# One-hot matrices of the gates: two tokens innermost instead of four

## The chip, the cores and the metric

The kernel runs on one core of a Trainium2 chip. The metric is the device time of one execution in microseconds (us); the lower the better. The kernel before takes 3132.16 us (median of 3 runs, 3129.18 to 3136.56).

## The reference, cut to what matters

The model is a small decoder of two layers over 512 tokens (and 16 meta tokens) of width 1024. The first layer mixes tokens by causal pooling, the second by stick-breaking attention; behind each stands a PEER feed-forward, which is what matters here:

```python
q = einsum('btd,dq->btq', hx, w_query)            # 8 heads, 2 halves of 128
s = einsum('bthpc,hpnc->bthpn', q, sub_keys)      # 128 sub-keys per half
top_s, top_i = lax.top_k(s, 16)                   # per half
cand_s = top_s[0][:, None] + top_s[1][None, :]    # 256 candidates
best_s, best_pos = lax.top_k(cand_s, 16)          # per head
gate = softmax(best_s)                            # expert = i1 * 128 + i2
act = gelu(einsum('btd,bthkd->bthk', hx, u[expert]))
y = einsum('bthk,bthkd->btd', gate * act, v[expert])
```

So each token picks 8 x 16 = 128 of 16384 experts, each named by two sub-keys i1 and i2 out of 128, with a gate.

## The kernel before, in words

**Tiling.** The 512 tokens are four blocks of 128. In each layer three of them are handled densely: for every one of the 128 values j of the first sub-key, the kernel computes gelu(u_e . h) for the 128 experts of that j and all 384 dense tokens (`u_parts`, a "u step" of 24 matmuls of 384 columns), multiplies by the gates, and accumulates with the v rows (`v_step`). The fourth block, and the meta tokens, gather their own rows by indirect DMA (`row_steps`: rows fetched by GpSimd, two DVE operations and one of ACT for each). Float32 matmuls are done as three fp32r matmuls of high and low parts: ACT makes a high part (`w_hi`, L279), DVE or GpSimd the low part (`w_lo`, L281 or L283).

**The gates as a dense matrix.** The dense form wants, for each token, a 128 x 128 matrix of gates: entry (i2, i1) is the gate of expert (i1, i2), nearly all zero. `build_gates` makes it for a block of 128 tokens. First the lists i1, i2 and gate are transposed on TensorE, so that the 128 picks of a token lie on the 128 partitions and the tokens along the free dimension (`sl`, 16-bit, with the gate in a high and a low part). Then the tokens are taken in groups of TG = 4, 32 groups for a block. For each group DVE makes four tiles of 128 partitions (picks) x 512 elements (128 key numbers x 4 tokens), fp16:

- L593: `ab[:, 0]` is 1 where the key number equals i2 (a compare of the constant `iota_x` with column 1 of `sl`, read again for every key number);
- L594: `e1` is 1 where the key number equals i1;
- L595 and L596: `ab[:, 1]` and `ab[:, 2]` are `e1` times the high and the low part of the gate.

`place` then multiplies, for each of the four tokens, the transposed one-hot of i2 by the two others and sums both into PSUM (`pg`, L574 and L576: eight matmuls of 128 x 128 x 128 a group). ACT copies `pg` to a staging tile (L581), and after 32 tokens a DMA writes that to memory (`gout`), from where the v steps read it back.

**How the four tokens lie.** In `ab` and `e1` the token is the innermost index: the 512 elements of a partition are 128 key numbers of 4 tokens each. A matmul takes one token, `ab[:, 0, :, q]`, so its weights (L574, L576: LDWEIGHTS) and its moving columns are read at a step of four fp16 elements, 8 bytes.

**What orders the work.** All engines run in program order. While gates are built (`pinned`, `gating`), a small planner in Python interleaves three streams with estimated costs: the DVE work of the gates (1.34 us for a group's builds, the selection's yields), quarters of u steps on TensorE (`ucost`), and row steps of the gathered tokens; a group's eight matmuls are counted with 0.5 us. The matmuls of a group are placed GLAG = 2 groups behind its builds; `ab` has three buffers, so the builds of group n wait until the matmuls of group n - 3 are done. u weights have two buffers: ACT splits the next weights when a u step has released one, and DVE's `w_lo` waits for that. In the last 16 groups of a layer no row steps are placed (QUIET). Behind the gates come the remaining u steps and all v steps. Ahead of each block's groups stands the selection (`select`, DVE: top 16, indices, softmax), in which L439 and L442 make other one-hot tiles in bf16 and f32.

Of the kernel before, what the change touches and what calls it, by code (L numbers as in the profile page):

```python
# [10 lines left out]
F16 = mybir.dt.float16  # L11
# [4 lines left out]
ALU = mybir.AluOpType  # L16
# [4 lines left out]
P = 128  # L21
# [6 lines left out]
NK = 128  # L28
# [11 lines left out]
TG = 4  # L40
GLAG = 2
# [16 lines left out]
def trunk_kernel(ctx: ExitStack, tc: tile.TileContext, x, meta, norm_mix, norm_ffn, pool_w, pool_scale,  # L58
                 kv_norm, w_kv, k_norm, w_q, q_norm, w_o, peer_wq, peer_keys, peer_ut, peer_uv, out):
    nc = tc.nc  # L60
    v, sc, pe, gp, sy = nc.vector, nc.scalar, nc.tensor, nc.gpsimd, nc.sync
# [4 lines left out]
    def const(shape, dt, name):  # L66
        return cp.tile(shape, dt, name=name)

    ident = const([P, P], F32, "ident")
    make_identity(nc, ident)  # L70
    iota_x = const([P, P, TG], F16, "iota_x")
    iota_b = const([P, TK], BF, "iota_b")
    own = const([P, AH], F32, "own")
    rr = const([P, H, NM], F32, "rr")
# [54 lines left out]
    def pool_mixer(gain, normed):  # L129
        with tc.tile_pool(name="pm", bufs=1, reuse_waits="tile") as s1, \  # L130
# [4 lines left out]
            iota_f = s1.tile([P, P], F32, name="iota_f")  # L135
            gp.iota(iota_f, pattern=[[1, P]], base=0, channel_multiplier=0, allow_small_or_imprecise_dtypes=True)
            pi = s1.tile([P, 1], I32, name="pi")
            gp.iota(pi, pattern=[[0, 1]], base=0, channel_multiplier=1)
            v.tensor_copy(iota_x, iota_f.unsqueeze(2).to_broadcast([P, P, TG]))
            v.tensor_copy(iota_b, iota_f[:, :TK])  # L140
            for op, n, name in ((ALU.logical_shift_right, 4, "head"), (ALU.bitwise_and, NM - 1, "slot")):
                pj = s1.tile([P, 1], I32, name=f"{name}_i")
# [112 lines left out]
    def peer(layer, with_meta, gain, hn_nat, kp, up, finish):  # L255
# [12 lines left out]
        with ExitStack() as cl:  # L268
# [21 lines left out]
            def pin(x):  # L290
                return tc.keep_in_program_order(x) if pinned[0] else x
# [90 lines left out]
            with ExitStack() as c1:  # L382
# [168 lines left out]
                gb = c1.enter_context(tc.tile_pool(name="gb", bufs=1, reuse_waits="tile"))  # L551

                def build_gates(n, i1, i2, gate):

                    pt = ps1.tile([P, 4, P], F32, name="ps1")
                    for q, t in enumerate((i1, i2, gate)):
                        pe.transpose(pt[:, q, :], t, ident)
                    sl = gb.tile([P, 4, P], F16, name="sl", bufs=2)
                    sc.activation(sl[:, :2], pt[:, :2], AF.Copy)
                    sc.activation(sl[:, 2], pt[:, 2], AF.Copy, scale=GSCALE)  # L560
                    gf = gb.tile([P, P], F32, name="gf")
                    v.tensor_copy(gf, sl[:, 2])
                    v.scalar_tensor_tensor(sl[:, 3], pt[:, 2], GSCALE, gf, ALU.mult, ALU.subtract)
                    stages = {}

                    def place(t0, ab):
                        tb = t0 // TB
                        if tb not in stages:
                            stages[tb] = gb.tile([P, NK, TB], F32, name="stage", bufs=2)
                        stage = stages[tb]  # L570
                        pg = ps1.tile([P, TG, NK], F32, name="pg")
                        with tc.issue_after(pmark[-1].ins):
                            for q in range(TG):
                                pin(pe.matmul(pg[:, q, :], ab[:, 0, :, q], ab[:, 1, :, q],  # L574
                                                 start=True, stop=False))
                                pin(pe.matmul(pg[:, q, :], ab[:, 0, :, q], ab[:, 2, :, q],  # L576
                                                 start=False, stop=True))
                        pcost[0] += 0.5
                        o = t0 % TB
                        with tc.issue_after(amark[-1].ins):  # L580
                            sc.activation(stage[:, :, o:o + TG].rearrange("p j t -> p t j"), pg, AF.Copy,  # L581
                                                  scale=1.0 / GSCALE)
                        if o + TG == TB:
                            sc.dma_start(gout[:, n * (P // TB) + tb], stage)

                    waiting = []
                    for t0 in range(0, P, TG):
                        ab = gb.tile([P, 3, NK, TG], F16, name="ab", bufs=GLAG + 1)
                        e1 = gb.tile([P, NK, TG], F16, name="e1", bufs=2)

                        def col(q):
                            return sl[:, q, t0:t0 + TG].unsqueeze(1).to_broadcast([P, NK, TG])
                        v.tensor_tensor(ab[:, 0], iota_x, col(1), ALU.is_equal)  # L593
                        v.tensor_tensor(e1, iota_x, col(0), ALU.is_equal)  # L594
                        v.tensor_tensor(ab[:, 1], e1, col(2), ALU.mult)  # L595
                        vmark.append(v.tensor_tensor(ab[:, 2], e1, col(3), ALU.mult))  # L596
                        waiting.append((t0, ab))
                        if len(waiting) > GLAG:
                            place(*waiting.pop(0))
                        yield 1.34  # L600
                    for wq in waiting:
                        place(*wq)
# [3 lines left out]
                def gate_stream():  # L606
                    if with_meta:
                        res = []
                        yield from select(gb, gr, "gm", tvm, tim, 1, res)
                        gather_rows(NT, 0, *res, TK, ym, True)  # L610
                    for n, i in enumerate(dense):
                        res = []
                        yield from select(gb, gb, "gd", tv[i], ti[i], H, res)
                        for cost in build_gates(n, *res):
                            blocks[0] -= 1
                            yield cost
# [392 lines left out]
    with tc.tile_pool(name="k0", bufs=1, reuse_waits="tile") as k0, \  # L1009
            tc.tile_pool(name="up", bufs=1, reuse_waits="tile") as up:  # L1010
        normed = {i: k0.tile([P, D], F32, name=f"hnat{i}") for i in (*GATHERED, NT)}
        gain = k0.tile([P, D], F32, name="gain")
        pool_mixer(gain, normed)
        peer(0, True, gain, normed, k0, up, lambda i, cs: None)
# [38 lines left out]
```

## Time and profile before

| | |
|---|---|
| median of 3 runs | 3132.16 us |
| profiled execution | 3127.99 us, of which the span is 3126.3 us |
| mean granted TensorE clock | 0.984 of full speed |
| gates of the first layer: first and last of their matmuls | 310.7 and 632.2 us |
| gates of the second layer: first and last of their matmuls | 2052.8 and 2372.1 us |
| PE, DVE, ACT, POOL busy, share of the span | 96%, 78%, 43%, 22% |
| HBM read and written | 673.99 and 81.53 MB |

PE is TensorE's matmuls, PEld its weight loads (they run beside the matmuls), DVE is VectorE, ACT ScalarE, POOL GpSimd. Times in the trace count from the start of the span. A matmul's duration holds its latency as well as its streaming, and matmuls are pipelined, so that the distance between two starts, not the duration, is what one costs. A wait is put down to the instruction whose end released it. L12 is line 12 of the kernel.

### The profile page before, as it was taken

The page shows a single profiled execution, that of the slowest core. Times are in us where ns is not written, and L with a number is a line of the kernel's source. Part 1 is how long each engine was busy: PE and PEld are TensorE (multiplying, and loading weights), DVE is VectorE, ACT ScalarE, POOL GpSimd, SP SyncE. Part 2 cuts the span into 40 slices and gives each one's busy share as a digit, 9 for nine tenths or more (in the row PEclk, how much of TensorE's full clock was granted, in tenths as well). Part 3 has the DMA queues.
Part 4 walks back from the last instruction along what each step waited for, and adds up shares of the span by engine and source line. Part 5 has one row for each costly group of instructions (what it writes and reads, how often), then busy time and mean ns, then how long its engine had stood idle before and what let it go on. Part 6 is the DMA issues. An engine that isn't in the chain of part 4 may idle for free.

```text
span 3126.3 us, 45813 instructions
## 1 busy us (share of the span) xinstructions
PE 2999.0 (96%) x16514; PEld 2671.7 (85%) x16514; DVE 2449.1 (78%) x5636; ACT 1354.3 (43%) x2184; POOL 688.7 (22%) x704
## 2 busy tenths in 40 slices
PE   8988999999999999999999989799999999999999
PEld 7887988988888888879965778798898888888887
DVE  3999998878777778786456469999987777777765
ACT  3443645643333333335455334354655333333333
POOL 3431311111111111114245244222110111111100
PEclk9999999999999999999999999999999999999999
DMA  3435877799989899762100344477878998989875
GB/s 134 179 121 202 282 265 265 274 360 329 338 312 321 314 329 329 273 245 90 55 1 1 108 177 144 158 262 269 303 253 326 358 314 321 331 308 333 307 250 164
DMA packets 286708, 758.52 MB, mean 243 GB/s; under 512 B 23184, under 2 KB 176784, under 8 KB 248336
## 3 DMA queue, kind: packets, MB, share of 16 engines
q1 hardware_dynamic: 222544, 390.92, 36.8%
q0 software_dynamic: 39168, 285.23, 24.9%
q10 hardware_dynamic: 24768, 79.44, 6.6%
q8 instruction: 129, 2.11, 0.3%
q14 instruction: 99, 0.81, 0.1%
HBM read 673.99 MB, written 81.53 MB: 242 GB/s over the span
## 4 chain that ended last, share of the span: by engine, by line
PE 77%; DVE 16%; DMA 3%; ACT 2%; issue 1%; POOL 0%; SPq 0%; DVEq 0%; ACTq 0%; POOLq 0%
PE y L690 31%; PE psu L314 27%; PE pg L574 3%; PE pg L576 3%; PE pp L124 2%; PE pp L125 2%; PE pp L123 2%; DVE mr L395 1%; DVE prod L355 1%; DVE w_lo L281 1%; DMA gt<-gout 1%; DVE ti L397 1%; DVE hx L367 1%; DMA w<-in_peer_ut_dram 1%; DVE ti L394 1%
## 5 line engine op out<-in xcount | busy, mean ns | idle before, releaser
L343 POOL DMA_INDIRECT row<-in_peer_uv_dram,ei x272 | 383.3, 1409 | 1833.1 <-DVE hx L367 1481.9
L314 PE MATMUL psu<-n_hi,w_lo 128*128 128x384 f32 x2048 | 701.5, 343 | 42.4 <-DVE w_lo L281 39.9
L314 PE MATMUL psu<-n_hi,w_hi 128*128 128x384 f32 x2048 | 720.4, 352 | 11.5 <-ACT ac L321 7.2
L314 PE MATMUL psu<-n_lo,w_hi 128*128 128x384 f32 x2048 | 703.0, 343 | 0.6 <-DVE n_lo L118 0.6
L279 ACT ACTIVATE w_hi<-w 128x1024 fp32r<-128x1024 f32 x288 | 305.6, 1062 | 467.7 <-PE psu L314 373.2
L690 PE MATMUL y<-v_lo,wt_hi 128*128 128x512 f32 x1536 | 473.6, 390 | 1.6 <-DVE v_lo L676 1.6
L690 PE MATMUL y<-v_hi,wt_hi 128*128 128x512 f32 x1536 | 473.8, 390 | 0.5 <-ACT v_hi L675 0.5
L690 PE MATMUL y<-v_hi,wt_lo 128*128 128x512 f32 x1536 | 473.6, 389 | 0.0
L314 PEld LDWEIGHTS psu<-n_hi,w_lo 128*128 128x128 f32 x2048 | 394.0, 192 | 49.0 <-DVE w_lo L281 45.8
L314 PEld LDWEIGHTS psu<-n_hi,w_hi 128*128 128x128 f32 x2048 | 395.4, 193 | 17.8 <-ACT ac L321 7.5
L314 PEld LDWEIGHTS psu<-n_lo,w_hi 128*128 128x128 f32 x2048 | 394.0, 192 | 5.5 <-DVE n_lo L118 1.1
L682 ACT ACTIVATE wt_hi<-wt 128x384 fp32r<-128x384 f32 x256 | 134.3, 525 | 574.0 <-PE y L690 295.5
L683 DVE TENSOR_TENSOR wt_lo<-wt,wt_hi 128x384 fp32r<-128x384 f32 x256 | 142.5, 557 | 264.3 <-ACT wt_hi L682 264.3
L281 DVE TENSOR_TENSOR w_lo<-w,w_hi 128x1024 fp32r<-128x1024 f32 x228 | 278.2, 1221 | 83.2 <-ACT w_hi L279 82.6
L690 PEld LDWEIGHTS y<-v_lo,wt_hi 128*128 128x128 f32 x1536 | 288.1, 188 | 63.3 <-DVE v_lo L676 2.9
L690 PEld LDWEIGHTS y<-v_hi,wt_lo 128*128 128x128 f32 x1536 | 288.3, 188 | 60.4
L355 DVE SCALAR_TENSOR_TENSOR prod<-row,hnat 128x1024 bf16<-128x1024 f32 x272 | 337.7, 1241 | 0.6 <-DMA row<-in_peer_uv_dram,ei 0.5
L367 DVE SCALAR_TENSOR_TENSOR hx<-row,gwt,hx 128x1024 f32<-128x1024 f32 x256 | 334.5, 1307 | 2.1
L690 PEld LDWEIGHTS y<-v_hi,wt_hi 128*128 128x128 f32 x1536 | 286.8, 188 | 52.8 <-ACT v_hi L675 0.9
L676 DVE TENSOR_TENSOR v_lo<-v,v_hi 128x1024 fp32r<-128x1024 f32 x256 | 312.2, 1219 | 5.4 <-ACT v_hi L675 5.2
L581 ACT ACTIVATE stage<-pg 128x512 f32<-128x512 f32 x192 | 216.9, 1137 | 149.2 <-PE pg L576 146.3
L675 ACT ACTIVATE v_hi<-v 128x1024 fp32r<-128x1024 f32 x256 | 270.8, 1058 | 10.6 <-DMA v<-in_peer_uv_dram 9.5
(313 smaller groups left out, 4695.0 us busy)
## 6 DMA issues: line engine op xcount, KB each, us to landing
w<-in_peer_ut_dram SPq DMA_DIRECT2D x256, 512.0 KB, 5.9
v<-in_peer_uv_dram SPq DMA_DIRECT2D x256, 512.0 KB, 6.1
gout<-stage ACTq DMA_DIRECT2D x24, 2048.0 KB, 8.4
gt<-gout SPq DMA_DIRECT2D x64, 768.0 KB, 10.2
aout<-ac ACTq DMA_DIRECT2D x148, 192.0 KB, 4.0
ac<-aout SPq DMA_DIRECT2D x148, 192.0 KB, 5.9
w<-in_peer_wq_dram SPq DMA_DIRECT2D x32, 512.0 KB, 3.4
wn<-in_w_kv_dram SPq DMA_DIRECT2D x8, 1024.0 KB, 5.5
```

The source lines that it names most:

```text
L279: amark.append(sc.activation(whi, w, AF.Copy))
L281: vmark.append(v.tensor_sub(wlo, w, whi.bitcast(F32)))
L314: m = pin(pe.matmul(ps[:, :ND], a[:, k, :], b[:, k, c0:c0 + ND], start=st, stop=en))
L343: gp.indirect_dma_start(out=row, out_offset=None, in_=peer_uv, in_offset=bass.IndirectOffsetOnAxis(ap=item[1], axis=0))
L355: v.scalar_tensor_tensor(prod, row[:, :D], 1.0, hn_nat[i], ALU.mult, ALU.mult, accum_out=dot)
L367: v.scalar_tensor_tensor(acc, row[:, D:], wt, acc, ALU.mult, ALU.add)
L581: sc.activation(stage[:, :, o:o + TG].rearrange("p j t -> p t j"), pg, AF.Copy, scale=1.0 / GSCALE)
L675: amark.append(sc.activation(vhi, v32, AF.Copy))
L676: vmark.append(v.tensor_sub(vlo, v32, vhi.bitcast(F32)))
L682: sc.activation(whi, wt, AF.Copy)
L683: vmark.append(v.tensor_sub(wlo, wt, whi.bitcast(F32)))
L690: pe.matmul(y[n][half], wp[:, ts], vq[:, half * 512:(half + 1) * 512], start=st, stop=en)
```

## The change

The token index is split in two: of the four tokens of a group, two stay innermost and the pairs become an outer index. `ab` changes from 3 x 128 x 4 to 3 x 2 x 128 x 2 elements a partition, `e1` and the constant `iota_x` follow, with the constant read twice by a broadcast over the pairs. Sizes of `ab` and `e1`, the number of instructions and their order stay. A matmul's operands are then read at a step of two fp16 elements, 4 bytes. In the DVE operations the operand from `sl` is read in runs of two tokens, each run repeated for 128 key numbers, where before it was runs of four.

```diff
-    iota_x = const([P, P, TG], F16, "iota_x")
+    iota_x = const([P, P, 2], F16, "iota_x")
-            v.tensor_copy(iota_x, iota_f.unsqueeze(2).to_broadcast([P, P, TG]))
+            v.tensor_copy(iota_x, iota_f.unsqueeze(2).to_broadcast([P, P, 2]))
...
                             for q in range(TG):
-                                pin(pe.matmul(pg[:, q, :], ab[:, 0, :, q], ab[:, 1, :, q],
+                                a, b = divmod(q, 2)
+                                pin(pe.matmul(pg[:, q, :], ab[:, 0, a, :, b], ab[:, 1, a, :, b],
                                                  start=True, stop=False))
-                                pin(pe.matmul(pg[:, q, :], ab[:, 0, :, q], ab[:, 2, :, q],
+                                pin(pe.matmul(pg[:, q, :], ab[:, 0, a, :, b], ab[:, 2, a, :, b],
                                                  start=False, stop=True))
...
-                        ab = gb.tile([P, 3, NK, TG], F16, name="ab", bufs=GLAG + 1)
-                        e1 = gb.tile([P, NK, TG], F16, name="e1", bufs=2)
+                        ab = gb.tile([P, 3, TG // 2, NK, 2], F16, name="ab", bufs=GLAG + 1)
+                        e1 = gb.tile([P, TG // 2, NK, 2], F16, name="e1", bufs=2)
+                        ix = iota_x.unsqueeze(1).to_broadcast([P, TG // 2, NK, 2])

                         def col(q):
-                            return sl[:, q, t0:t0 + TG].unsqueeze(1).to_broadcast([P, NK, TG])
-                        v.tensor_tensor(ab[:, 0], iota_x, col(1), ALU.is_equal)
-                        v.tensor_tensor(e1, iota_x, col(0), ALU.is_equal)
+                            pair = sl[:, q, t0:t0 + TG].rearrange("p (a b) -> p a b", b=2)
+                            return pair.unsqueeze(2).to_broadcast([P, TG // 2, NK, 2])
+                        v.tensor_tensor(ab[:, 0], ix, col(1), ALU.is_equal)
+                        v.tensor_tensor(e1, ix, col(0), ALU.is_equal)
```

## Rows read from the trace of the kernel before

**Rows 1.** The page: busy us, share of the span and instructions of each engine.
```profile
PE 2999.0 (96%) x16514; PEld 2671.7 (85%) x16514; DVE 2449.1 (78%) x5636; ACT 1354.3 (43%) x2184; POOL 688.7 (22%) x704
```
**Rows 2.** The page: the chain that ended last, by engine and by line.
```profile
PE 77%; DVE 16%; DMA 3%; ACT 2%; issue 1%; POOL 0%; SPq 0%; DVEq 0%; ACTq 0%; POOLq 0%
PE y L690 31%; PE psu L314 27%; PE pg L574 3%; PE pg L576 3%; PE pp L124 2%; PE pp L125 2%; PE pp L123 2%; DVE mr L395 1%; DVE prod L355 1%; DVE w_lo L281 1%; DMA gt<-gout 1%; DVE ti L397 1%; DVE hx L367 1%; DMA w<-in_peer_ut_dram 1%; DVE ti L394 1%
```
**Rows 3.** Busy by stretch: window, length, engines (instructions), clock, DMA share, GB/s.
```profile
310.00:400.00 90.00, 87.69 (x582) 82.03 (x580) 84.77 (x241) 56.23 (x68) 31.54 (x8) 1.00 0.82 294
425.00:520.00 95.00, 89.41 (x583) 82.92 (x582) 87.22 (x236) 55.84 (x70) 18.34 (x7) 0.98 0.72 261
560.00:640.00 80.00, 78.59 (x529) 72.93 (x527) 66.39 (x156) 50.58 (x59) 12.43 (x5) 1.00 0.77 278
sum 265.00, PE 255.69 PEld 237.88 DVE 238.38 ACT 162.66 POOL 62.30; mean PE 85.23 PEld 79.29 DVE 79.46 ACT 54.22 POOL 20.77
...
sum 241.00, PE 238.02 PEld 221.29 DVE 222.20 ACT 150.75 POOL 42.57; mean PE 79.34 PEld 73.76 DVE 74.07 ACT 50.25 POOL 14.19
...
720.00:780.00 60.00, 60.00 (x292) 53.24 (x291) 47.38 (x69) 23.89 (x39) 9.24 (x8) 1.00 0.89 313
```
**Rows 4.** Timeline of PE at a group's end: start us, us, instruction.
```profile
444.31 0.30 PE L576 MATMUL pg<-ab 128*128 128x128 f16 x1
...
444.78 0.29 PE L576 MATMUL pg<-ab 128*128 128x128 f16 x1
444.83 0.42 PE L314 MATMUL psu<-n_hi,w_hi 128*128 128x384 f32 x1
```
**Rows 5.** Groups by line and shape: busy us, mean ns of one, idle before.
```profile
L314 PE MATMUL psu<-n_lo,w_hi 128*128 128x384 f32 x2048 | 703.0, 343 | 0.6 <-DVE n_lo L118 0.6
L690 PE MATMUL y<-v_hi,wt_hi 128*128 128x512 f32 x1536 | 473.8, 390 | 0.5 <-ACT v_hi L675 0.5
L576 PE MATMUL pg<-ab 128*128 128x128 f16 x768 | 192.7, 297 | 0.0
L123 PE MATMUL pp<-wn_hi,n_hi 128*128 128x256 f32 x384 | 110.9, 289 | 0.1
L574 PEld LDWEIGHTS <-ab 128*128 128x128 f16 x768 | 89.2, 116 | 30.8 <-issue 16.3 <-DVE ab L595 4.5 <-DVE e L594 3.1
L593 DVE TENSOR_TENSOR ab<-iota_x,sl 128x512 f16<-128x512 f16 x192 | 80.5, 419 | 20.9 <-PE pg L576 20.2
L442 DVE TENSOR_TENSOR oh<-oh,tib 128x2048 bf16<-128x2048 bf16 x12 | 14.6, 1218 | 0.0
L884 PE MATMUL z<-negm,ident_b 128*128 128x128 bf16 x64 | 14.0, 219 | 0.0
L439 DVE TENSOR_TENSOR oh<-iota_b,db 128x2048 bf16<-128x2048 bf16 x6 | 13.7, 2282 | 0.0
L884 PEld LDWEIGHTS <-ident_b 128*128 128x128 bf16 x64 | 6.3, 99 | 2.5
```
**Rows 6.** DVE's waits in each layer's gates, then in a selection stretch of each.
```profile
DVE w_lo L281 <- ACT w_hi L279: 14.5, 15, 3.0
DVE ab L593 <- PE pg L576: 10.5, 17, 1.2
DVE gwt L363 <- ACT ga L359: 3.1, 1, 3.1
...
DVE w_lo L281 <- ACT w_hi L279: 12.1, 13, 3.0
DVE ab L593 <- PE pg L576: 9.7, 18, 1.6
DVE gwt L363 <- ACT ga L359: 2.0, 1, 2.0
...
DVE w_lo L281 <- ACT w_hi L279: 6.8, 5, 3.0
...
DVE w_lo L281 <- ACT w_hi L279: 6.3, 4, 3.0
```

## The prediction

> **What bounds the kernel now.** I read the page's busy line first: PE 96%, so the array is the suspect [rows 1]. The chain of waits agrees: PE holds 77% of the path, DVE 16%, and the two lines of the gate matmuls 3% each [rows 2]. Six per cent of 3126 us is some 190 us, so the place of the change is on the path. The question is what else is nearly on it there. The busy times by stretch answer that [rows 3]. The gates of one layer are built in three blocks, one for each dense token block, with a stretch of top-16 selection ahead of each. In the six gate stretches together (506 us) PE is busy 255.69 + 238.02 = 493.7 us (98%), DVE 238.38 + 222.20 = 460.6 us (91%), ACT 313.4 us (62%). PE binds, and DVE has 45.4 us of idle time in all: that is the room a faster PE can use before DVE binds.
>
> What a gate matmul costs is read from start times, since a duration holds the latency as well. From 444.31 to 444.78 us there are four steps: 117.5 ns each [rows 4]. A group of four tokens has eight such matmuls, 0.94 us, and there are 2 x 3 x 32 = 192 groups with 768 matmuls on each of two lines [rows 5].
>
> **The change part by part.** No instruction is added, removed or moved. The queues keep their order, since the planner's costs (0.5 for a group's matmuls, 1.34 for its builds) stay as written. What changes is the address step of the operands.
>
> *Moving operand, 8 bytes to 4.* The trace has no 16-bit operand at a step of 4 bytes, so I bound it by neighbours. The fp32r matmuls read dense 4-byte elements, which is a step of 4 bytes: 289 ns at 256 columns, 343 at 384, 390 at 512, so 128 more columns cost 54 or 47 ns, about 51 [rows 5]. A dense bf16 matmul of 128 columns lasts 219 ns where the gate matmul lasts 297: 78 ns more for the same shape [rows 5]. If the reading is what stretches it, the pitch falls from 117.5 to between 51 (columns alone) and 67 (117.5 - 51, two columns where one was read), and if it is not, it stays at 117.5. I take 65, near the fp32r row, because that row has the very step that the change makes: 52 ns less, 0.42 us less for a group, 192 x 0.42 = 81 us of PE time in all. Ends kept for the range: 0 and 0.53 us a group.
>
> *Weight loads, 8 bytes to 4.* The gate loads last 116 ns, a dense bf16 load 99 [rows 5]. They run beside the matmul before them; I count 0, at most 17 ns each, and a rival below is about the case where they are what binds.
>
> *The one-hot builds on DVE.* Four operations a group, 768 in all, 418 ns each for 512 elements [rows 5]. That is the faster of two rates the trace shows: 2048 bf16 elements took 1218 ns where all operands are 16-bit, and 2282 ns where one is f32 [rows 5]. The per-token column was read as runs of four tokens, repeated for each key; now it is a run of two, one 4-byte word, read 128 times over before the next. The 2282 ns row is of that kind: its f32 operand is one 4-byte word repeated 16 times, and it goes at (2282 - 1218) / 1024 = 1.04 ns a word with no penalty to be seen. So I keep 418. Bounds: 0, and 266 ns more each (1064 / 4, the slower rate).
>
> *ACT's copy out of PSUM* and the DMAs of the gates read the same tiles as before: 0. The constant with the key numbers gets half as long; it is cast once at the start of the kernel, off the path.
>
> **From PE time to time.** PE's 81 us cannot all be had: about 40 us a layer, against a DVE idle of 26.6 us in the first layer's three stretches and 18.8 us in the second's [rows 3]. DVE is what is late next. How much of its idle time hangs on PE is read from its waits [rows 6]. In the first layer DVE waits 14.5 us for the high parts of the u weights (ACT makes them, itself held until PE has released a buffer), 10.5 us for gate matmuls to release the one-hot tile, and 3.1 us for an ACT operation of the gathered rows; in the second 12.1, 9.7 and 2.0. Of the w_lo waits 6.8 and 6.3 us lie in a selection stretch, where PE runs u matmuls only and nothing gets faster. That leaves 28.1 + 23.8 - 13.1 = 38.8 us. Not all will go: the ACT split itself takes its time, and in 425 to 520 us PE too has 5.6 us of idle time [rows 3], so the two engines hold each other up by turns there. I take three quarters, 30 us; the ends are 15 (only the direct waits for gate matmuls, 10.5 + 9.7 = 20.2, and not all of these) and 45 (all of DVE's idle time). Because DVE ends it, the exact pitch matters little: 80 ns would still free 0.3 us a group, 58 us, above the 38.8.
>
> The stage behind the gates is bound by PE (60.00 busy of 60 us at 720 to 780 [rows 3]), so what the gates give up arrives at the end of the kernel. The profiled execution took 3127.99 us: 3128 - 30 = 3098. The median of the runs shown lies 4 us above the profiled one: 3102.
>
> **Rivals.** *The pitch is not the reading* (no effect, 3132; with a little, 3120). If the array waits for weights, or if a step of 8 bytes is already free, the 117.5 ns stay. For it: the fp32r matmul behind the last gate matmul of a group starts 50 ns after it, not 117 [rows 4], as if those 128 columns had gone through at the rate of dense ones, and its own duration is drawn out to 420 ns. Against it: the loads are just 17 ns longer than dense ones, so loads at a small step and at a large one differ by about what reading would explain. If loads bind and lose these 17 ns, PE saves 17 x 8 x 192 = 26 us, of which I would expect under half, 12.
>
> [...]
>
> *DVE loses its rate* (slower). If the run of two drops the builds to the slower rate, each takes 684 ns: 768 x 0.266 = 204 us more on an engine with 45.4 us of room, so 204 - 45 = 159 us longer, 3291 us. It decides from 45.4 / 768 = 59 ns an operation, that is above 477 ns; below that PE still hides it. Against it is the repeated word at full rate above; for it, that no row has a run of two.
>
> [...]
>
> **How the numbers follow.** The forecast, with times from 3085 to 3118, gets 0.60. The first rival gets 0.28, a fifth of it with a gain that can be told from none. The second gets 0.09, and 0.03 is left for a slower run without a cause named here. A measurement of this kernel tells about 0.2% (6.3 us) from no change. Faster: 0.60 + 0.06 = 0.66; within 0.2%: 0.24; slower: 0.10. The range goes from 3084 (all of DVE's idle time, from the median) to 3136, which takes in the case of no effect; it leaves out DVE at a lower rate.
>
> **What would show it.** Right: gate matmuls start 51 to 80 ns apart and last about 220 to 245 ns; DVE's wait for them (20.2 us in both layers) falls below 5 us; DVE is busy 96% or more in the gate stretches; PE's share there falls; the builds stay at 418 ns. The first step is wrong if the pitch stays above 110 ns; the DVE step if a build is over 477 ns; the conversion if the pitch falls and DVE still shows 30 us or more of idle time, because ACT or the buffers of the u weights hold it. A granted clock under the 1.00 and 0.98 of the gate stretches [rows 3] would mean that PE, less busy, is slowed in turn.

## The result, and the profile after

The kernel after takes 3102.85 us (median of 4 runs, 3101.14 to 3109.71), against 3131.34 us of the kernel before on the same chip: a ratio of 0.9911, 95% interval 0.9891 to 0.9930. The forecast was 3102. The profiled execution took 3103.72 us, 24.3 less than the one of before (3127.99). In the kernel after, the lines of the u steps and of `w_lo` keep their numbers; L574, L576, L581, L593 to L596 and L690 of before are L575, L577, L582, L596 to L599 and L693.

Timeline of PE in the kernel after, at the end of a group (start us, us, instruction), against [rows 4]:

```profile
444.98 0.22 PE L577 MATMUL pg<-ab 128*128 128x128 f16 x1
445.04 0.22 PE L575 MATMUL pg<-ab 128*128 128x128 f16 x1
...
445.32 0.22 PE L577 MATMUL pg<-ab 128*128 128x128 f16 x1
445.35 0.42 PE L314 MATMUL psu<-n_hi,w_hi 128*128 128x384 f32 x1
```

From 444.98 to 445.32 there are six steps: 57 ns each, where [rows 4] gave 117.5. Groups by line and shape of the kernel after (busy us, mean ns of one, idle before and its releasers), against [rows 5]:

```profile
L577 PE MATMUL pg<-ab 128*128 128x128 f16 x768 | 110.1, 221 | 3.1 <-DVE ab L599 0.5
L575 PEld LDWEIGHTS <-ab 128*128 128x128 f16 x768 | 72.5, 98 | 45.2 <-issue 21.9 <-DVE ab L598 13.1 <-DVE ab L599 4.0
L596 DVE TENSOR_TENSOR ab<-iota_x,sl 128x512 f16<-128x512 f16 x192 | 80.4, 419 | 2.1 <-PE pg L577 1.9
L598 DVE TENSOR_TENSOR ab<-e,sl 128x512 f16<-128x512 f16 x192 | 80.4, 419 | 0.0
L314 PE MATMUL psu<-n_hi,w_lo 128*128 128x384 f32 x2048 | 705.9, 345 | 64.4 <-DVE w_lo L281 62.4 <-POOL w_lo L283 2.0
```

The last of these rows in the kernel before:

```profile
L314 PE MATMUL psu<-n_hi,w_lo 128*128 128x384 f32 x2048 | 701.5, 343 | 42.4 <-DVE w_lo L281 39.9 <-POOL w_lo L283 2.4
```

The matmul lasts as long as the dense bf16 one did (221 against 219 ns [rows 5]), the weight load as well (98 against 99), and a build stays at 419 ns. What DVE waited for gate matmuls went from 20.2 to 1.9 us. The last row has the wait that grew: PE stands 62.4 us for the low parts of the u weights, which DVE makes (39.9 in the kernel before). DVE has gained weight on the path, and the page says so, in its busy line and its chain, against [rows 1, 2]:

```profile
PE 2942.2 (95%) x16514; PEld 2605.9 (84%) x16514; DVE 2446.9 (79%) x5636; ACT 1349.8 (44%) x2184; POOL 734.9 (24%) x704
...
PE 68%; DVE 26%; DMA 2%; issue 2%; ACT 2%; POOL 0%; SPq 0%; DVEq 0%; ACTq 0%; POOLq 0%
PE y L693 33%; PE psu L314 21%; DVE w_lo L281 3%; PE pp L124 2%; PE pp L125 2%; PE pp L123 2%; DVE prod L355 2%; DVE ab L599 2%; DVE ab L598 2%; DVE e L597 2%; DVE hx L367 2%; DVE ab L596 2%; DVE mr L395 1%; DVE ti L397 1%; DVE ti L394 1%
```

The gate matmuls have left the lines shown of the chain; the four builds have come in with 2% each, and the row steps (L355, L367) and `w_lo` went from 1% each to 2 and 3%. DVE's share went from 16 to 26%, PE's from 77 to 68%. Busy time in the six stretches of gate matmuls, each block from its first to its last, summed (columns as in [rows 3]); first the kernel before, then the kernel after:

```profile
sum 461.10, PE 452.46 PEld 419.14 DVE 424.70 ACT 293.51 POOL 100.02; mean PE 75.41 PEld 69.86 DVE 70.78 ACT 48.92 POOL 16.67
```

```profile
sum 419.00, PE 386.32 PEld 345.36 DVE 412.53 ACT 286.74 POOL 145.30; mean PE 64.39 PEld 57.56 DVE 68.76 ACT 47.79 POOL 24.22
```

DVE is busy 412.53 of 419.0 us (98%), PE 386.32 (92%); before it was 92 and 98% of 461.1 us. Last, the whole stage of gates, from its first to its last gate matmul, in both layers; first the kernel before, then the kernel after:

```profile
310.70:632.20 321.50, 308.47 (x1970) 290.07 (x1969) 294.27 (x719) 183.60 (x229) 68.89 (x25) 0.98 0.76 272
2052.80:2372.10 319.30, 307.93 (x1971) 289.77 (x1970) 295.03 (x718) 182.51 (x229) 56.73 (x25) 0.98 0.75 272
```

```profile
309.20:611.10 301.90, 275.36 (x1970) 253.03 (x1970) 291.19 (x718) 181.34 (x229) 93.16 (x25) 0.97 0.80 286
2041.80:2345.90 304.10, 277.18 (x1971) 255.19 (x1970) 290.96 (x716) 179.31 (x229) 80.52 (x25) 0.96 0.80 284
```

The stages hold nearly the same instructions, and are 19.6 and 15.2 us shorter, 34.8 in all. DVE's idle time in them (length less busy) went from 27.2 + 24.3 = 51.5 to 10.7 + 13.1 = 23.8 us, 27.7 less; PE's rose from 24.4 to 53.5. Time left PE and was got back little further than DVE had stood idle. The other 7.1 of the 34.8 us are a fall of DVE's busy time; the durations of its operations add up to the same there (691.8 and 690.3 us), so most of it is that neighbours overlap in the record where a gap had parted them.

### The profile page after: what moved, and what is told of

Read it like the earlier page. It is cut to its first block, busy times and chain, and to the rows that moved or that the text cites. A ratio compares the mean times of both kernels' runs of the same rounds, so it can differ in the third digit from the quotient of the medians.

```text
span 3102.0 us, 45813 instructions
## 1 busy us (share of the span) xinstructions
PE 2942.2 (95%) x16514; PEld 2605.9 (84%) x16514; DVE 2446.9 (79%) x5636; ACT 1349.8 (44%) x2184; POOL 734.9 (24%) x704
## 4 chain that ended last, share of the span: by engine, by line
PE 68%; DVE 26%; DMA 2%; issue 2%; ACT 2%; POOL 0%; SPq 0%; DVEq 0%; ACTq 0%; POOLq 0%
PE y L693 33%; PE psu L314 21%; DVE w_lo L281 3%; PE pp L124 2%; PE pp L125 2%; PE pp L123 2%; DVE prod L355 2%; DVE ab L599 2%; DVE ab L598 2%; DVE e L597 2%; DVE hx L367 2%; DVE ab L596 2%; DVE mr L395 1%; DVE ti L397 1%; DVE ti L394 1%
## 5 line engine op out<-in xcount | busy, mean ns | idle before, releaser
L343 POOL DMA_INDIRECT row<-in_peer_uv_dram,ei x272 | 429.0, 1577 | 1751.3 <-DVE hx L367 1406.2
L314 PE MATMUL psu<-n_hi,w_lo 128*128 128x384 f32 x2048 | 705.9, 345 | 64.4 <-DVE w_lo L281 62.4
L314 PE MATMUL psu<-n_hi,w_hi 128*128 128x384 f32 x2048 | 722.2, 353 | 11.5 <-ACT ac L321 7.2
L314 PE MATMUL psu<-n_lo,w_hi 128*128 128x384 f32 x2048 | 706.0, 345 | 0.6 <-DVE n_lo L118 0.6
L693 PE MATMUL y<-v_hi,wt_hi 128*128 128x512 f32 x1536 | 474.0, 390 | 1.2 <-ACT wt_hi L685 0.8
L693 PE MATMUL y<-v_hi,wt_lo 128*128 128x512 f32 x1536 | 473.9, 390 | 0.2
L693 PE MATMUL y<-v_lo,wt_hi 128*128 128x512 f32 x1536 | 473.5, 389 | 0.5 <-DVE v_lo L679 0.5
L314 PEld LDWEIGHTS psu<-n_hi,w_lo 128*128 128x128 f32 x2048 | 396.5, 194 | 73.5 <-DVE w_lo L281 71.1
L314 PEld LDWEIGHTS psu<-n_hi,w_hi 128*128 128x128 f32 x2048 | 394.9, 193 | 17.5 <-ACT ac L321 7.5
L314 PEld LDWEIGHTS psu<-n_lo,w_hi 128*128 128x128 f32 x2048 | 395.3, 193 | 5.5 <-DVE n_lo L118 1.1
L693 PEld LDWEIGHTS y<-v_lo,wt_hi 128*128 128x128 f32 x1536 | 288.2, 188 | 61.8 <-DVE v_lo L679 1.3
L693 PEld LDWEIGHTS y<-v_hi,wt_lo 128*128 128x128 f32 x1536 | 288.1, 188 | 61.3 <-DVE wt_lo L686 1.1
L367 DVE SCALAR_TENSOR_TENSOR hx<-row,gwt,hx 128x1024 f32<-128x1024 f32 x256 | 334.5, 1307 | 2.1
L355 DVE SCALAR_TENSOR_TENSOR prod<-row,hnat 128x1024 bf16<-128x1024 f32 x272 | 335.7, 1234 | 0.4 <-DMA row<-in_peer_uv_dram,ei 0.4
L693 PEld LDWEIGHTS y<-v_hi,wt_hi 128*128 128x128 f32 x1536 | 286.6, 188 | 54.1 <-ACT wt_hi L685 1.4
L582 ACT ACTIVATE stage<-pg 128x512 f32<-128x512 f32 x192 | 211.7, 1133 | 103.5 <-PE pg L577 102.4
```

The source lines that it names most:

```text
L314: m = pin(pe.matmul(ps[:, :ND], a[:, k, :], b[:, k, c0:c0 + ND], start=st, stop=en))
L343: gp.indirect_dma_start(out=row, out_offset=None, in_=peer_uv, in_offset=bass.IndirectOffsetOnAxis(ap=item[1], axis=0))
L355: v.scalar_tensor_tensor(prod, row[:, :D], 1.0, hn_nat[i], ALU.mult, ALU.mult, accum_out=dot)
L367: v.scalar_tensor_tensor(acc, row[:, D:], wt, acc, ALU.mult, ALU.add)
L693: pe.matmul(y[n][half], wp[:, ts], vq[:, half * 512:(half + 1) * 512], start=st, stop=en)
```

## The experiments

Two questions were open. The first: is the pitch (the distance between two starts) of 117.5 ns the reading of the moving columns, as forecast, or the weight loads, and what is the rule? The second: does DVE end the gain, so that PE's time no longer counts?

### Which operand it is

**e1_moving4.** Only the two moving tiles and `e1` lie in pairs; the weights keep their step of 8 bytes.

```diff
-ab = gb.tile([P, 3, TG // 2, NK, 2], F16, name="ab", bufs=GLAG + 1)
+ab = gb.tile([P, 3, NK * TG], F16, name="ab", bufs=GLAG + 1)
...
+def byp(i):
+    return ab[:, i].rearrange("p (a n b) -> p a n b", a=TG // 2, b=2)[:, a, :, b]
+def byq(i):
+    return ab[:, i].rearrange("p (n t) -> p n t", t=TG)[:, :, q]
+pin(pe.matmul(pg[:, q, :], byq(0), byp(1), start=True, stop=False))
+pin(pe.matmul(pg[:, q, :], byq(0), byp(2), start=False, stop=True))
```

> Only the moving operands (the two one-hots times the gate) and e1 lie in pairs of tokens; the weights stay at a step of 8 bytes. Theory: the pitch of the gate matmuls is the reading of the moving columns, so it is 57 to 62 ns as in the changed kernel while the weight loads stay at 112 to 117 ns; DVE is again what is late, so 3100 to 3108 us. Rival (the weights' step sets the pitch): 115 to 118 ns and 3128 to 3136 us. The constant of the key numbers is kept in fours and read in runs of two at a step of 8 bytes, so the build of e1 may show whether DVE minds that; both theories expect 418 ns.

Measured: 3107.33 us, ratio 0.9915 (0.9898 to 0.9931). Timeline of PE and the weight loads of this kernel:

```profile
441.76 0.22 PE L581 MATMUL pg<-ab 128*128 128x128 f16 x1
...
442.12 0.22 PE L581 MATMUL pg<-ab 128*128 128x128 f16 x1
442.14 0.42 PE L314 MATMUL psu<-n_hi,w_hi 128*128 128x384 f32 x1
```

```profile
L581 PEld LDWEIGHTS <-ab 128*128 128x128 f16 x768 | 91.2, 119 | 0.7 <-issue 0.7
```

Six steps in 0.36 us are 60 ns, while a load still lasts 119. So loads of 119 ns go beside matmuls 60 ns apart: the length of a load is not its price. The whole gain is there (0.9915 against 0.9911), though the builds are recorded with 432 to 433 ns here; they still start 335 ns apart, as in the kernels before and after. The theory of the moving operand holds, that of the loads falls.

**e2_weights4.** The other half: only the weights lie in pairs.

```diff
+pin(pe.matmul(pg[:, q, :], byp(0), byq(1), start=True, stop=False))
+pin(pe.matmul(pg[:, q, :], byp(0), byq(2), start=False, stop=True))
```

> The reverse: only the weights lie in pairs of tokens, the moving operands stay at a step of 8 bytes. Theory (moving columns set the pitch): weight loads fall to 97 to 99 ns, the pitch stays at 110 to 118 ns, 3126 to 3134 us. Rival (weights set it): pitch 57 to 62 ns, 3100 to 3108 us. If the two halves each did part of it, pitches between these and times in between.

Measured: 3134.81 us, ratio 0.9999 (0.9989 to 1.0008). Timeline and weight loads:

```profile
442.83 0.30 PE L581 MATMUL pg<-ab 128*128 128x128 f16 x1
...
443.54 0.30 PE L581 MATMUL pg<-ab 128*128 128x128 f16 x1
443.58 0.43 PE L314 MATMUL psu<-n_hi,w_hi 128*128 128x384 f32 x1
```

```profile
L581 PEld LDWEIGHTS <-ab 128*128 128x128 f16 x768 | 87.0, 113 | 0.4
```

Six steps in 0.71 us: 118 ns, and no gain. The time was as expected; the load was not, since it kept 113 ns at a step of 4 bytes. Its duration beside a slow stream doesn't tell its own step.

### The rule of the step

**e3_dense.** The token goes outermost, so that each operand is read at 2 bytes; in the builds the column operand is then one fp16 element held for 128 keys.

```diff
-ab = gb.tile([P, 3, TG // 2, NK, 2], F16, name="ab", bufs=GLAG + 1)
+ab = gb.tile([P, 3, TG, NK], F16, name="ab", bufs=GLAG + 1)
...
-    return pair.unsqueeze(2).to_broadcast([P, TG // 2, NK, 2])
+    return sl[:, q, t0:t0 + TG].unsqueeze(2).to_broadcast([P, TG, NK])
```

> The token outermost, so that all operands of the matmuls are dense (a step of 2 bytes) and the per-token column of the builds is one element repeated for 128 keys. Theory: the array gains nothing over a step of 4 bytes (pitch 55 to 58 ns, loads 97 to 99 ns), but the builds fall to the slower rate, 684 ns each, and as DVE was already what is late, nearly all of 768 x 0.266 = 204 us arrives: 3280 to 3310 us. Rival: the repeated element keeps the faster rate, 418 ns, and the time is that of the changed kernel, 3100 to 3108. Second rival: a step of 2 bytes is faster again (pitch under 50 ns); with DVE late it would show in the pitch alone.

Measured: 3295.95 us, ratio 1.0508 (1.0491 to 1.0526). Two groups of this kernel:

```profile
L594 DVE TENSOR_TENSOR ab<-iota_x,sl 128x512 f16<-128x512 f16 x192 | 135.7, 707 | 0.8 <-ACT sl L559 0.8
L574 PE MATMUL pg<-ab 128*128 128x128 f16 x768 | 131.9, 229 | 107.6 <-DVE ab L596 104.5 <-ACT ac L321 1.4 <-ACT w_hi L279 0.9
```

Each build takes 707 ns instead of 419 by its record, and PE waits 104.5 us for one of them alone. Timelines of two builds and of a group's matmuls:

```profile
480.33 0.70 DVE L596 TENSOR_TENSOR ab<-e,sl 128x512 f16<-128x512 f16 x1
480.93 0.71 DVE L597 TENSOR_TENSOR ab<-e,sl 128x512 f16<-128x512 f16 x1
```

```profile
481.74 0.22 PE L574 MATMUL pg<-ab 128*128 128x128 f16 x1
...
482.02 0.22 PE L576 MATMUL pg<-ab 128*128 128x128 f16 x1
```

Builds start some 600 ns apart (602 in the median), where they started 335 apart in the kernels before and after: 267 ns more, which is what the slope of [rows 5] gave (266). The size agrees with the way in which the prediction worked out its slower rival: 768 x 0.267 = 205 us more DVE work, less its idle time of 51.5, is 154; 160 were measured. Five steps of the matmuls in 0.28 us are 56 ns; the median in this trace is 55, against 58 in the kernel after, so dense columns bring next to nothing more.

**e4_moving16.** The two moving tiles are interleaved, a step of 16 bytes; the builds write in blocks of four. The question is whether the pitch, 57 ns at 4 bytes and 118 at 8, rises further with the step.

```diff
+mv = gb.tile([P, NK, 2, TG], F16, name="mv", bufs=GLAG + 1)
...
-                                pin(pe.matmul(pg[:, q, :], ab[:, 0, a, :, b], ab[:, 1, a, :, b],
+                                pin(pe.matmul(pg[:, q, :], ab[:, :, q], mv[:, :, 0, q],
```

> The two moving operands interleaved, so that their columns lie 16 bytes apart; weights stay at 8 bytes. [...]

Measured: 3301.2 us (one run), 165 more than before. Timeline of PE, and the build that waits for it:

```profile
477.17 0.41 PE L576 MATMUL pg<-mv,ab 128*128 128x128 f16 x1
...
478.55 0.41 PE L576 MATMUL pg<-mv,ab 128*128 128x128 f16 x1
478.60 0.54 PE L314 MATMUL psu<-n_hi,w_hi 128*128 128x384 f32 x1
```

```profile
L594 DVE TENSOR_TENSOR ab<-iota_x,sl 128x512 f16<-128x512 f16 x192 | 81.5, 425 | 136.3 <-PE pg L576 135.5
```

Six steps in 1.38 us: 230 ns, twice the pitch at 8 bytes. DVE now waits 135.5 us for gate matmuls. Where PE binds, its time counts almost in full: 1536 matmuls x 112 ns are 172 us, and 165 came out. In the kernel after, 1536 x 60.5 ns = 93 us fewer brought 28.

**e5_step24.** Doubling from 4 over 8 to 16 bytes leaves two laws: time by the bytes swept, or by the units touched (16 bytes, the smallest size that the doubling allows). A step of 24 bytes (three tiles interleaved) parts them.

```diff
+ab = gb.tile([P, NK, 3, TG], F16, name="ab", bufs=GLAG + 1)
...
-                                pin(pe.matmul(pg[:, q, :], ab[:, 0, a, :, b], ab[:, 1, a, :, b],
+                                pin(pe.matmul(pg[:, q, :], ab[:, :, 0, q], ab[:, :, 1, q],
```

> The three one-hot tiles interleaved by key number, so that both weights and moving columns lie 24 bytes apart (the run with 16 bytes between moving columns had a pitch of 230 ns, with 8 bytes 118, with 4 bytes 57). Theory L (a column costs what its 16-byte line costs, 1.8 ns, shared by the columns that lie in it): beyond 16 bytes each column has a line of its own and nothing is added, pitch 225 to 245 ns, about 3300 us. Theory P (the cost goes with the bytes swept, 0.11 ns a byte): pitch 330 to 360 ns, about 3450 to 3520 us.

Measured: 3305.32 us (one run). Timeline of PE:

```profile
478.37 0.41 PE L574 MATMUL pg<-ab 128*128 128x128 f16 x1
...
479.54 0.41 PE L576 MATMUL pg<-ab 128*128 128x128 f16 x1
479.59 0.54 PE L314 MATMUL psu<-n_hi,w_hi 128*128 128x384 f32 x1
```

Five steps in 1.17 us: 234 ns, against 230 at 16 bytes, and far from the 330 to 360 of the other law (the weights lay 24 bytes apart here too). The pitch doubles with the step up to 16 bytes (57, 118, 230 ns) and rises no further at 24 (234), so from 4 bytes on it goes by units of 16 bytes:

| step of the moving columns | pitch of 128 columns | columns in 16 bytes | ns for 16 bytes |
|---|---|---|---|
| 2 bytes (e3_dense) | 55 ns | 8 | 3.4 (0.43 a column) |
| 4 (after, e1_moving4) | 57 to 60 | 4 | 1.8 to 1.9 (0.45 to 0.47 a column) |
| 8 (before, e2_weights4) | 118 | 2 | 1.8 |
| 16 (e4_moving16) | 230 | 1 | 1.8 |
| 24 (e5_step24) | 234 | 1 | 1.8 |

The same traces hold a second test of this, since the granted TensorE clock falls for short stretches from 1.00 to 0.50 of full speed. A group of the kernel before at a granted clock of 0.50 (509.9 to 513.2 us), and one of the kernel after (454.5 to 457.9 us):

```profile
512.26 0.30 PE L576 MATMUL pg<-ab 128*128 128x128 f16 x1
...
512.97 0.29 PE L576 MATMUL pg<-ab 128*128 128x128 f16 x1
```

```profile
455.29 0.31 PE L577 MATMUL pg<-ab 128*128 128x128 f16 x1
...
455.93 0.31 PE L577 MATMUL pg<-ab 128*128 128x128 f16 x1
```

Six steps each: 118 ns at a step of 8 bytes, as at the full clock, and 107 ns at 4 bytes, where the full clock gives 57. e4_moving16 keeps its 230 ns at 0.50 (561.4 to 571.5 us), and e3_dense goes from 55 to 107. So at 8 and 16 bytes the pitch does not follow TensorE's clock, and the columns' own rate (at 0.50, 107 ns for 128 of them) is not what sets it; at 2 and 4 bytes it does follow.

### What the time still hangs on

**mm1_before and mm1_after.** The second matmul of each token is left out, in either layout: the gates then lack their low part. PE gets half the gate matmuls; DVE's work stays.

```diff
-                 start=True, stop=False))
-pin(pe.matmul(pg[:, q, :], ab[:, 0, a, :, b], ab[:, 2, a, :, b],
-                 start=False, stop=True))
+                 start=True, stop=True))
```

> The kernel before with the second matmul of each token left out (the low part of the gate is missing from the result): four matmuls a group at the old pitch of 118 ns, so PE is spared 0.47 us a group, 90 us in all, nearly what the change spares (8 x 61 ns = 0.49 us, 94 us) by quite another edit. Theory (the gain is PE time in the gates, cut off where DVE becomes late): the same time as the changed kernel, 3098 to 3109 us. Rival (the gain has another source, the weight loads or the reads of the tiles): it differs from 3103 by more than 8 us.

> The changed kernel with the same matmul left out: PE is spared another 4 x 57 ns a group, 44 us in all. Theory (DVE is late): 0 to 10 us below the changed kernel, 3092 to 3104 us. Rival (PE still binds and the gain was cut by something else): 25 us or more below, under 3078.

Measured: 3097.08 us, ratio 0.9896 (0.9880 to 0.9913), and 3099.65, 0.9904 (0.9888 to 0.9921). Halving the gate matmuls of the old layout brings what the change brings (the time lies 1 us under the range that was expected); halving them once more in the new layout brings 0.9904 against 0.9911, nothing that can be told apart. The first layer's gate stage in mm1_after:

```profile
309.40:609.60 300.20, 258.07 (x1588) 233.97 (x1587) 290.64 (x718) 178.91 (x229) 104.79 (x25) 0.96 0.81 288
```

PE is busy 258.07 us where the kernel after had 275.36; DVE 290.64 against 291.19; and the stage is 300.20 us long against 301.90. So the theory that DVE ends it holds: PE's time has stopped counting.

**dve3_before and dve3_after.** The fourth build is left out: the low part of the gates isn't made, and the high part is read twice. By the distance of two starts that takes 192 x 0.335 = 64 us off DVE; PE's work stays.

```diff
-v.tensor_tensor(ab[:, 1], e1, col(2), ALU.mult)
-vmark.append(v.tensor_tensor(ab[:, 2], e1, col(3), ALU.mult))
+vmark.append(v.tensor_tensor(ab[:, 1], e1, col(2), ALU.mult))
```

> The kernel before without the fourth build (the low part of the gate is not made; the second matmul reads the high part again, so PE has the same work): DVE is spared some 0.335 us a group, 64 us in all. Theory (PE binds before the change): little of it arrives, 0 to 18 us, 3114 to 3133 us. Rival (both engines hold each other up, so either one's time counts): 25 us or more.

> The changed kernel without the fourth build. Theory (DVE is late after the change): most of the 64 us arrives until PE binds again, 30 to 55 us, 3048 to 3073 us. Rival (the rest of PE's idle time is held by ACT or the two buffers of the u weights): less than 15 us, above 3088.

Measured: 3126.76 us, ratio 0.9983 (0.9973 to 0.9993), and 3073.13, 0.9820 (0.9804 to 0.9837). DVE's busy time on the page fell by 55.3 us in the old layout (2449.1 to 2393.8) and by 53.5 in the new (2446.9 to 2393.4). The same relief of DVE is worth 7 us in the old layout and, by the ratios (0.9911 to 0.9820), 28 in the new. DVE's waits in the first gate stage, in dve3_before (us, times, longest), show where it goes in the old layout:

```profile
DVE ab L593 <- PE pg L576: 27.6, 36, 1.6
```

The wait for gate matmuls rises to 27.6 us in this layer, from 10.5 [rows 6]: DVE, with less to do, stands before PE. The new layout gives 28 of some 54 us, a little under the range that was expected (30 to 55). The stage of dve3_after:

```profile
311.50:601.30 289.80, 270.27 (x1970) 251.50 (x1969) 263.20 (x623) 180.37 (x229) 53.01 (x25) 0.98 0.83 299
```

PE is busy 93% there and DVE 91%. Once DVE is relieved, neither fills the stage. In this stretch PE waits 15.2 us for DVE's `w_lo`, DVE 15.1 us for ACT's `w_hi`, and ACT 39.0 us for PE's u matmuls to release the buffer: they hold each other up through the u weights. No run took this ring apart.

### Can DVE's share be made smaller?

DVE still has room behind the gates (47 of 60 us [rows 3]), so its row steps could be moved there. Three changes of the planner's numbers alone tried it, all on the kernel after. **plan_slack** has the first of these two edits, which lets the planner fill more time beside the gates; **rows_only** has the second, which places row steps further apart while gates are built and closer in the v stage; **plan_rows** has both.

```diff
-DVE_SLACK = 1.08
+DVE_SLACK = 1.2
...
-ROW_PERIOD = ((18.0, 13.5), (18.0, 13.5))
+ROW_PERIOD = ((26.0, 11.5), (26.0, 11.5))
```

> The changed kernel with the planner's factor on DVE's costs raised from 1.08 to 1.2, so that more u steps are placed beside the same builds. Theory (in the gates DVE is late and PE has some 60 us of idle time in both layers): a u step takes 4.2 us of PE out of the stage behind and costs DVE 1.2 us here, so 3065 to 3090 us. Rival (the u weights' two buffers hold PE up however many steps are placed): 3098 to 3108 us.

> As the run before, and fewer gathered rows in the query and gate stages (a step of them each 26 / 8 us of planned time, was 18 / 8) and more in the v stage (11.5 / 8, was 13.5 / 8), where DVE has idle time. Theory: DVE is spared some 15 rows x 2.6 us a layer where it is late, 3040 to 3075 us, faster than the run before. Rival (the v stage has no room: its row fetches and v loads hold PE): slower than the run before.

> The changed kernel with the fewer gathered rows in the query and gate stages, and the planner's factor left at 1.08. The run with both edits took 3091 us, the one with the factor alone 3101, the changed kernel 3103. Theory (what helps is the DVE time taken out of the stages where DVE is late; extra u steps give nothing, as each brings 1.2 us of DVE work to that stage): 3086 to 3096 us. Rival (the rows help only with the extra u steps): 3097 to 3106 us.

Measured: plan_slack 3101.29 us, 0.9890 (0.9873 to 0.9906); plan_rows 3091.24, 0.9858 (0.9842 to 0.9875); rows_only 3106.77, 0.9912 (0.9896 to 0.9929). The page counts the stores of finished u steps, one for each u step placed beside the gates; first the kernel after, then plan_slack, plan_rows and rows_only:

```profile
aout<-ac ACTq DMA_DIRECT2D x148, 192.0 KB
```

```profile
aout<-ac ACTq DMA_DIRECT2D x164, 192.0 KB
```

```profile
aout<-ac ACTq DMA_DIRECT2D x149, 192.0 KB
```

```profile
aout<-ac ACTq DMA_DIRECT2D x134, 192.0 KB
```

More slack alone puts 16 more u steps beside the gates: the first stage takes 327.6 us instead of 301.9, the stretch behind the second 727.8 instead of 756.1, and the sum stays; the theory that those steps come for nothing fell. The time is the one that the rival gave, but its reason is not shown: DVE is busy 306.97 of the 327.6 us and PE 302.89, so both engines have idle time there, and no run tells whether the two buffers are what makes it. Fewer row steps alone lower the DVE time that the planner counts, so 14 fewer u steps are placed, and those run later; here the theory fell and the rival's account held. Only both together keep the u steps (149) and take rows out. The first layer's gate stage in plan_rows:

```profile
303.60:602.20 298.60, 278.74 (x1994) 258.75 (x1993) 275.45 (x679) 181.95 (x225) 55.81 (x17) 0.96 0.73 262
```

POOL's count says 17 row fetches where there were 25, and DVE's busy time fell by 16 us; the stage got only 3.3 us shorter (10.6 in the second layer), and it started 5.6 us earlier (303.6 instead of 309.2), since row steps were taken out ahead of it too; the stretches behind the two stages took 2.1 and 2.2 us longer. The direction was right and the size was missed by far (3040 to 3075 expected). plan_rows is the fastest complete version, by ratio 0.9858 against 0.9911 of the kernel after, though the two were timed beside different runs of the kernel before.

## Why the prediction was right, point by point

**The moving operand.** Taken 65 ns, bounds 51 and 117.5; measured 57. The middle bound of 67 is no result of "two columns where one was read": that would be half of 117.5, 59, and near what came out. The neighbour chosen, dense fp32r with its step of 4 bytes, was the right one, and e1_moving4 and e2_weights4 show that the moving operand alone carries it. By the pitch 93 us of PE time were freed (1536 x 60.5 ns) where the sum had 81; but PE's busy time on the page fell by 56.8 only. A part of that is the clock: by the trace's records it stood at 0.50 of full speed for 99.4 us before and for 133.9 after, and an estimate from that is up to 17 us more of PE time (half of the 34.5). It shows in the gate matmuls themselves (107 ns at 0.50, above) and in the u matmuls (in the kernel after two starts are 0.32 us apart at 0.50, at 454.52 and 454.84 us, and 0.18 at 1.00, at 308.29 and 308.47): the three groups of L314 held 701.5 + 720.4 + 703.0 us before and 705.9 + 722.2 + 706.0 after, 9.2 more. The rest was not traced.

**The rival "the pitch is not the reading"** got 0.28, in part on evidence that was none: the fp32r matmul behind the last gate matmul starts 50 ns after it. In the timelines above it starts 20 to 50 ns after it whether the pitch is 60, 118, 230 or 234. So the recorded start of the next matmul does not say that the stream before it has ended. The matmul after that one says more: from the last gate matmul to it are 285 ns at 4 bytes, 311 at 8 and 423 at 16 (medians). From 8 to 16 bytes that is 112 ns more, as much as the pitch grew, so this part of the cost stands in the record of the successor. The rival's other condition, that a step of 8 bytes is already free, did not hold either: 118 ns at 8 bytes, two columns in 16, and 57 at 4, four columns in 16.

**Weight loads counted at 0.** Right, and now shown: 119 ns loads at a pitch of 60. Whether the 3 ns between this and the 57 of the kernel after belong to the weights is not shown.

**The builds at 418 ns.** Right: 419, and 335 from start to start as before. The repeated f32 word of [rows 5] was the fitting neighbour for a pair of fp16 repeated 128 times. e3_dense shows that the danger was real one step further: a single fp16 repeated takes 707 ns. It also puts the reading of L439 in doubt: that row has an f32 operand and one element repeated next to each other, and e3_dense goes at the slower rate without any f32, so the f32 need not be what makes L439 slow.

**PE time into time.** The step that carried the number was that DVE is late next. It is shown by the two pairs: less PE work is worth 37 us before and nothing that can be told after, less DVE work (some 54 us) 7 us before and 28 after. Of DVE's idle time 30 us were to go; over the two whole stages 27.7 went. The parts: the wait for gate matmuls went as forecast (20.2 to 1.9, "below 5"), and that for the high parts of the u weights fell less than counted. DVE's waits in the kernel after, first and second layer's gate stage from first to last gate matmul:

```profile
DVE w_lo L281 <- ACT w_hi L279: 9.1, 6, 3.0
DVE ab L596 <- PE pg L577: 1.1, 2, 0.9
...
DVE w_lo L281 <- ACT w_hi L279: 11.6, 8, 3.0
DVE ab L596 <- PE pg L577: 0.8, 2, 0.7
```

They add up to 20.7 us for `w_lo`. From first to last gate matmul the kernel before has 14.5 and 13.0 (12.1 for the second layer in [rows 6]): 6.8 us less, where the sum of 38.8 had 13.5 in it.

**The conversion to the end.** "What the gates give up arrives at the end" held by part. The stages are 34.8 us shorter in the profiled executions, the span 24.3. The stretch between the two layers' gates, with the same instructions, took 1430.7 us instead of 1420.6; the stretch behind the second took 756.1 instead of 754.2. One wait of PE makes 4.8 of the 10.1 us, that for DVE's `n_lo` (us, times, longest); first the kernel before, then the kernel after:

```profile
PE pt L115 <- DVE n_lo L118: 2.3, 2, 1.6
```

```profile
PE pt L115 <- DVE n_lo L118: 7.1, 2, 5.5
```

It adds up to 5.1 us in e2_weights4 and to 7.5 in dve3_before, whose gates hardly moved and whose stretch between took 1424.8 and 1426.3 us: so it does not hang on the gain in the gates. Another 3.5 us are PE's busy time (1370.1 to 1373.6), with the clock at 0.50 for 47.8 us there instead of 41.0. By medians the gain is 28.5.

That the forecast met the median to 1 us is in part luck. The stages gave 34.8 us where 30 were forecast, the way to the end took 10.5 back where nothing was, and the 4 us by which the median was to lie above the profiled execution did not come (it lies 0.9 below).

**Sums that do not close.** All of DVE's idle time from the median is 3132 - 45 = 3087, not the 3084 of the range. The two slower cases have 0.09 + 0.03 = 0.12 where the sum has 0.10, and four fifths of 0.28 are 0.22 where it has 0.24. The six gate stretches of [rows 3], 506 us, reach past the gate matmuls (461.1 us from the first to the last of each block). None of this moves the forecast.

**The clock.** The prediction named a granted clock under 1.00 and 0.98 as a sign that PE, less busy, is slowed in turn. The lower clock is there. Before, and then after, in the stretch from 440 to 480 us:

```profile
440.00:480.00 40.00, 38.56 (x258) 35.65 (x258) 36.81 (x92) 26.04 (x31) 11.29 (x4) 1.00 0.74 269
```

```profile
440.00:480.00 40.00, 34.28 (x249) 30.63 (x248) 38.46 (x98) 22.99 (x29) 11.07 (x4) 0.91 0.88 315
```

PE was busy 34.28 us instead of 38.56, and for a part of the stretch got 0.50 of the full clock (mean 0.91); in the 14.5 us ahead of the first fall (440.0 to 454.5) it was busy 11.34. This stretch is among the worst: over the whole stages the granted clock went from 0.98 and 0.98 (PE busy 96% in both) to 0.97 and 0.96 (91% in both); mm1_after has 0.96 and 0.95 (86% in both), but the second stage of mm1_before 0.98 with 90%. That PE's idle time is the cause was not shown. DVE, busy 38.46 of 40, covers the lower clock there. How much of it reaches the end was not measured apart.

## What to carry to other kernels

Where one dimension of a tile is picked out by a matmul (shown here for fp16), lay the tile so that the moving columns lie at most 4 bytes apart (57 ns for 128 columns, against 118 at 8 bytes); where the operation that writes it needs runs to keep its rate, make the runs two fp16 elements long and no longer (a build of 419 ns, against 707 with single elements). Count a faster engine's gain by the idle time of the engine that is late next, in the stage of the change, and not by the time freed: here 93 us freed gave 28. Then look at what the planner gives that engine to do there, and change its budget and its work together, since either alone only moves work.

## What was not expected of the hardware

- The moving operand cost 1.8 ns for each 16 bytes touched, with one, two or four of its columns in them, and with eight the pitch was 0.43 ns a column at the full clock: 55, 57, 118, 230 and 234 ns for 128 columns at 2, 4, 8, 16 and 24 bytes.
- At 8 and 16 bytes the pitch did not change with TensorE's granted clock (118 and 230 ns at 0.50 too); at 2 and 4 bytes it went from 55 and 57 to 107 ns.
- A weight load's recorded length (98 to 149 ns) went with its own step (98 ns at 4 bytes in the kernel after, 114 and 119 at 8 in e1_moving4, both beside a fast stream) and with the stream beside it: 113 ns at 4 bytes beside a slow stream, 98 beside a fast one. In none of these runs did it set the pitch, but for 3 ns that are open (60 against 57).
- The matmul behind a strided stream shows a start 20 to 50 ns after it and a drawn-out duration of its own (0.42 to 0.43 us behind pitches of 57 to 118, 0.54 behind 230 and 234; 0.34 elsewhere), so a part of a stream's cost stands in the record of its successor.
- DVE's builds of fp16 took 419 ns where the broadcast operand came in pairs and 707 where it came as single elements, at the same number of elements. By the distance of starts it is 335 and 602; the durations overlap, and the 267 ns between them are what the slope of [rows 5] gave.
